# Writing out the order of an FFN's last sums and the next mixer's first tiles, moving one score span to other PSUM banks, and reordering a mixer's end

## The chip, the cores and the metric

The kernel runs on one core of one Trainium2 chip. The metric is the device time in microseconds of one execution. Before the change the median of three runs is 1155.68 us (1155.24 to 1155.77).

A core has five engines that run at the same time, each in the order of its own queue: TensorE (PE in the profile, its weight loads PEld), VectorE (DVE), ScalarE (ACT), GpSimd (POOL) and SyncE (SP), which here only sends DMAs. They wait for one another through semaphores. TensorE writes its sums to PSUM, which has eight banks of 128 partitions by 512 float32.

## The reference: what is computed

The reference is a decoder trunk of two layers on 512 tokens of width 1024. Each layer is a mixer (attention) and a gated convolutional FFN, both inside a residual with a norm ahead of it and a norm behind it:

```
h = rms_norm(x, pre_g);      x = x + rms_norm(mixer(h), post_g)
h = rms_norm(x, ffn_pre_g);  x = x + rms_norm(conv_ffn(h), ffn_post_g)
conv_ffn: u = dwconv(h @ w_up);  (silu(gate) * up) @ w_down
```

Layer 0 mixes with latent and differential attention. Layer 1 mixes with dilated attention in three head groups and with stick-breaking attention, whose scores are z = q k^T and whose weights are exp(log_sigmoid(z) + a reversed cumulative sum of log_sigmoid(-z)) below the diagonal.

## The kernel before: how the work is laid out

The 512 tokens are four rows of 128 tokens each, X[0] to X[3], held with tokens on the partitions. ORDER = (3, 2, 1, 0) is the order in which rows are finished and taken up. A normed row has to be turned (transposed by TensorE, eight 128x128 blocks in two groups of four) before it can be multiplied, since a product contracts over partitions.

Products that need precision are done in three parts. A value is split into a high part (a cast by ScalarE) and a low part (a subtraction by VectorE), and `mm3` (L259 to L263) adds high x high, high x low and low x high into one PSUM bank: three matmuls of 128x512.

**Weights.** The class `Weights` (L39) keeps a list of all weights in the order of use. `load` sends a DMA of 512 KB into one of three raw buffers, `_emit` splits it (ScalarE L73, VectorE L74) into one of five pairs wh, wl, and `next` hands out a pair after making sure that `depth` units from the present one are made.

**The planner.** Instructions are laid out on each engine by a planner with its own estimate of times, which may put a later instruction ahead of an earlier one that is not ready. Inside `tc.manual_schedule(engines={...})` the instructions that the program traces on the named engines keep the order in which they are written. SyncE is not among the named ones; and instructions that are written outside may still be put between.

**The first FFN's end** (in `ffn`, L555 to L568). The down projection is a product of 2x2 block matrices done with seven products in place of eight. Six banks are left at the end, a, b and c for two halves s = 0 and 1 of the tokens, and each takes its last TAIL = 4 units (12 matmuls). Out of a and of uu - b comes row 3 (s = 0) or row 1 (s = 1); out of uu - c and an earlier sum comes row 2 or row 0. `close` does for each row:

1. `residual` (L241): per half a square with a sum on ScalarE (L228), a product with the gain on VectorE (L223), for some halves a subtraction ahead (L220); `rstd` (L172) makes the factor on GpSimd with three operations on one column (L176, L178, L179); then the row's update on VectorE (L250).
2. `normalise` (L193): a square of the new row on ScalarE (L186), `rstd` with two operations, and two halves of the normed row on VectorE (L199).
3. `turned` (L203): per half four transposes (L209), a cast (ScalarE, L169) and a subtraction (VectorE, L170) into xh and xl.

In the kernel before this stretch is not written out: the planner lays it out.

**The second mixer** (`odd`, L1210). It starts with the value tiles of the two dilated groups (L1269 to L1283): for each row in ORDER eight `mm3` over the turned rows and four weights, a copy by ScalarE out of the bank, and four DMAs into `cv12`, sent from ScalarE's queue. The two turns that the FFN left over are popped in the middle of these tiles. Then come the stick-breaking projections (`proj_T`, L1237, and `proj_V`, L1252), whose sums go to the three banks with tag a.

`sb_scores` (L1295) makes the scores of two heads in three spans of columns. Each span has one bank per head, by tag "ss", "nt", "ss", as "s" has two banks and "n" and "t" one each; VectorE adds the mask while it empties them (L1307). `sb_softplus` and `sb_weights` follow, the last with products with a triangle (L1334), each after a few projections that fill the time.

**The mixer's end** (L1534 to L1564), in a manual order on four engines: per row two half sums of the output projection, `part_of` for each half, the row's factor and update; the square of the row before it, its normed row (L1530), and its turn come between them, one or two rows later. The FFN that follows takes rows 3 and 2 first and pops the last two turns in its first products.

The lines that the steps of the prediction touch are L73, L74 (split of a weight), L169, L170 (split of a turned half), L176 to L179 (factor), L186, L228 (squares), L199, L1530 (normed), L209 (turn), L220, L223, L250 (half row and update), L261 to L263 (`mm3`), L1283 (stores of the value tiles), L1303, L1307 (scores and mask) and L1334 (triangle).

Of the kernel before, what the change touches and what calls it, by code (L numbers as in the profile page):

```python
# [17 lines left out]
P = 128  # L18
# [20 lines left out]
class Weights:  # L39
# [35 lines left out]

    def ahead(self, n):
        while len(self.made) < min(len(self.units), n):
            self._emit()
# [9 lines left out]
def trunk(tc, A, out):  # L88
# [3 lines left out]
    with ExitStack() as top:  # L92
# [5 lines left out]
        GAP = 24  # L98
# [83 lines left out]
        def mean_square(src, eps=epst):  # L182
            w = src.shape[1]
            junk = chp.tile([P, D], BF16, tag="junk", name="junk", bufs=1)
            ms = chp.tile([P, 1], F32, tag="ms", name="ms", bufs=4)
            ACT.activation(junk[:, :w], src, AF.Square, scale=w ** -0.5, accum_out=ms[:])  # L186
            return rstd(ms[:], None, eps)
# [50 lines left out]
        def begin_sum():  # L238
            return chp.tile([P, 2], F32, tag="ms", name="ms2", bufs=4)
# [104 lines left out]
        def ffn(layer, xnT, pending, final):  # L344
            with ExitStack() as es:
# [209 lines left out]
                def close(i, cs, at=None):  # L555
                    turns.append(normalise(i, g_next, nx, "tn", residual(i, cs, g_post, None, at)))

                for s in range(2):
                    for m in "abc":
                        for n in range(TAIL):  # L560
                            later_product(m, s, HF - TAIL + n, ws[n])
                        if m == "b":
                            close(3 - 2 * s, (bk["a", s], (uu[:, s], bk["b", s])))
                        if m == "c":
                            close(2 - 2 * s, ((uu[:, s], bk["c", s]), None), early_q[s])
                        if len(turns) > 1 and s == 1 and m != "c":
                            turns.pop(0)()
                return nx, turns  # L568
# [641 lines left out]
        def odd(xnT, pending):  # L1210
            xh, xl = xnT
            with ExitStack() as es:
# [6 lines left out]
                nc.scalar.dma_start(tab12[:], A["dil_tab12"])  # L1219
# [3 lines left out]
                ob = ap.tile([P, 4, 4, 66], F32, tag="ob", name="ob")  # L1223
                on = ap.tile([P, NT, 4, 66], F32, tag="on", name="on")
# [44 lines left out]

                ws = [W.next() for _ in range(4)]  # L1270
                for i in ORDER:
                    t = slice(i * P, (i + 1) * P)
                    a = bank("a", "av12")
                    for k in range(KD):
                        if k == KD // 2 and pending:
                            pending.pop(0)()
# [3 lines left out]
                    st = sb.tile([P, 512], F32, tag="sp", name="vst", bufs=2)  # L1280
                    ACT.copy(st[:], a[:])
                    for r in range(4):
                        nc.scalar.dma_start(cv12[32 * i:32 * i + 32, r], st[r::4, :])  # L1283
# [250 lines left out]
                norms, turns = [], []  # L1534
                with tc.manual_schedule(engines={PE.engine, DVE.engine, ACT.engine, POOL.engine}):
                    for n, i in enumerate(ORDER):
# [19 lines left out]
                        turns.append(turned(i, nx, "na", t))  # L1556

                    r = mean_square(X[i][:])

                def turn_next():  # L1560
                    turns[0]()
                    normed(i, r, t)
# [106 lines left out]
```

## Time and profile before

| | |
|---|---|
| median of 3 runs | 1155.68 us |
| the profiled execution's own time | 1155.71 us |
| its span, first to last instruction | 1153.9 us |
| mean granted TensorE clock | 0.998 |
| DVE, ACT, POOL busy | 71%, 48%, 6% of the span |

How to read it: a row of the timeline has the start in us from the span's start, the length in us, the engine, the line, the operation, out<-in by the program's names, the shapes and how many instructions were merged; in brackets stands how long the engine was idle ahead of it and what ended that. A row of groups has busy time, mean ns of one, and the idle time ahead with its releasers. A row of the table of stretches has the stretch, its length, the busy time and number of instructions of PE, PEld, DVE, ACT and POOL, the granted clock, the DMA engines' busy share and GB/s. Matmuls are pipelined, so the length of one (0.39 us for 128x512) is more than the distance to the next one's start; the ends are modelled. A tile is listed under the name it was made with, digits at its end dropped: `cv12` is cv, `zp` stays zp.

### The profile page before, as it was taken

To read this page: it belongs to the slowest core of one execution; us is meant where nothing else is said; L and a number is where in the kernel's file an instruction comes from. 1 tells how busy PE (TensorE), PEld (TensorE's weight loads), DVE (VectorE), ACT (ScalarE), POOL (GpSimd) and SP (SyncE) were. 2 spreads that over 40 slices of the span, in tenths; PEclk is the share of its full clock that TensorE was granted. 3 is DMA by queue.
4 is the path that set the end of the run, shared out by engine and by line. 5 is a ranking of instruction groups with operands and counts; after the bars stand their busy time and mean duration, and the time that the engine had idled before them with its cause. 6 is when DMAs were issued, how large, how long until landed. Compare 5 with 4: busy or idle time off the path is not lost.

```text
span 1153.9 us, 15139 instructions
## 1 busy us (share of the span) xinstructions
PE 1136.1 (98%) x5632; PEld 932.3 (81%) x5632; DVE 813.9 (71%) x1435; ACT 552.2 (48%) x935; POOL 71.1 (6%) x148
## 2 busy tenths in 40 slices
PE   9999999999999999999999999999999999999997
PEld 8766677898888888888778877888988888888886
DVE  5687686568667668889863564576676666679896
ACT  5555454444434444556543554454533433445562
POOL 3200123100000000000120000002000000000002
PEclk9999999999999999999999999999999999999999
DMA  8520132153333332455635223323233333324461
GB/s 309 170 67 19 50 92 89 64 168 110 92 92 106 94 91 76 129 153 180 203 122 163 63 69 92 92 57 110 77 110 107 95 91 98 103 82 139 143 210 73
DMA packets 40921, 128.38 MB, mean 111 GB/s; under 512 B 5008, under 2 KB 7696, under 8 KB 40848
## 3 DMA queue, kind: packets, MB, share of 16 engines
q1 hardware_dynamic: 37920, 123.08, 34.2%
q10 hardware_dynamic: 2928, 4.35, 1.2%
q8 instruction: 44, 0.72, 0.3%
q14 instruction: 29, 0.24, 0.1%
HBM read 119.53 MB, written 6.29 MB: 109 GB/s over the span
## 4 chain that ended last, share of the span: by engine, by line
PE 45%; issue 2%; DVE 1%; POOL 1%; ACT 1%; POOLq 0%; DVEq 0%; ACTq 0%
PE u L262 7%; PE u L263 7%; PE u L261 7%; PE acc L261 3%; PE acc L263 3%; PE acc L262 3%; PE apt L261 3%; PE apt L262 3%; PE apt L263 3%; PE cp L1334 1%; PE apv L261 1%; PE apv L263 1%; PE apv L262 1%; PE o L1418 1%; PE o L1495 1%
## 5 line engine op out<-in xcount | busy, mean ns | idle before, releaser
L74 DVE TENSOR_TENSOR wl<-wraw,wh 128x1024 fp32r<-128x1024 f32 x176 | 213.9, 1223 | 179.3 <-ACT wh L73 174.8
L73 ACT CAST wh<-wraw 128x1024 fp32r<-128x1024 f32 x176 | 182.8, 1048 | 264.6 <-PE u L262 179.3
L262 PE MATMUL u<-xl,wh 128*128 128x512 f32 (+1 forms) x768 | 285.7, 372 | 0.1
L263 PE MATMUL u<-xh,wl 128*128 128x512 f32 (+1 forms) x768 | 285.6, 372 | 0.0
L261 PE MATMUL u<-xh,wh 128*128 128x512 f32 (+1 forms) x768 | 285.3, 372 | 0.1
L261 PEld LDWEIGHTS u<-xh,wh 128*128 128x128 f32 x768 | 144.5, 188 | 25.5 <-ACT xh L169 0.6
L262 PEld LDWEIGHTS u<-xl,wh 128*128 128x128 f32 x768 | 144.7, 188 | 25.1 <-DVE xl L170 0.3
L263 PEld LDWEIGHTS u<-xh,wl 128*128 128x128 f32 x768 | 144.7, 188 | 24.9
L262 PE MATMUL acc<-wl,gh 128*128 128x512 f32 (+1 forms) x250 | 97.0, 388 | 0.0
L263 PE MATMUL acc<-wh,gl 128*128 128x512 f32 (+1 forms) x250 | 97.0, 388 | 0.0
L261 PE MATMUL acc<-wh,gh 128*128 128x512 f32 (+1 forms) x250 | 96.9, 389 | 0.0
L415 ACT ACTIVATE y<-y 128x512 f32<-128x512 f32 x44 | 27.7, 632 | 85.3 <-DVE y L413 85.3
L410 ACT ACTIVATE y<-u,cw 128x512 f32<-128x512 f32 x88 | 67.5, 774 | 1.7 <-PE u L263 1.7
L413 DVE SCALAR_TENSOR_TENSOR y<-u,cw,y 128x510 f32<-128x510 f32 x88 | 65.6, 747 | 2.5
L411 DVE SCALAR_TENSOR_TENSOR y<-u,cw,y 128x511 f32<-128x511 f32 x88 | 65.2, 744 | 0.9 <-ACT y L410 0.9
L176 POOL TENSOR_TENSOR rv<-ms,epst 128x1 f32<-128x1 f32 x27 | 7.6, 284 | 895.9 <-ACT junk L228 843.6
L591 ACT ACTIVATE s<-s,st 128x128 f32<-128x128 f32 (+3 forms) x64 | 35.8, 559 | 45.5 <-DVE st L589 28.2
L261 PEld LDWEIGHTS acc<-wh,gh 128*128 128x128 f32 x250 | 47.0, 188 | 10.1 <-issue 0.6
L262 PEld LDWEIGHTS acc<-wl,gh 128*128 128x128 f32 x250 | 47.0, 188 | 9.6
L263 PEld LDWEIGHTS acc<-wh,gl 128*128 128x128 f32 x250 | 47.0, 188 | 9.6
L261 PE MATMUL apt<-xh,wh 128*128 128x512 f32 x128 | 50.7, 396 | 0.0
L262 PE MATMUL apt<-xl,wh 128*128 128x512 f32 x128 | 50.1, 391 | 0.0
(328 smaller groups left out, 1985.8 us busy)
## 6 DMA issues: line engine op xcount, KB each, us to landing
wraw<-in_ffn_w_up SPq DMA_DIRECT2D x88, 512.0 KB, 3.6
wraw<-in_ffn_w_down SPq DMA_DIRECT2D x44, 512.0 KB, 3.7
wraw<-in_od_w_dqk SPq DMA_DIRECT2D x12, 512.0 KB, 3.6
wraw<-in_ffn_w_down SPq DMA_DIRECT2D x22, 256.0 KB, 2.7
wraw<-in_ev_w_dqk SPq DMA_DIRECT2D x8, 512.0 KB, 3.6
wraw<-in_ev_w_out SPq DMA_DIRECT2D x8, 512.0 KB, 3.6
spill<-X SPq DMA_DIRECT2D x8, 512.0 KB, 2.8
X<-spill SPq DMA_DIRECT2D x8, 512.0 KB, 6.3
```

The costliest lines, as they stand in the source:

```text
L73: self.nc.scalar.copy(h[:, :w], raw[:, :w])
L74: self.nc.vector.tensor_tensor(l[:, :w], raw[:, :w], h[:, :w].bitcast(F32), ALU.subtract)
L261: PE.matmul(o, lh, rh, start=first, stop=False, skip_group_check=more)
L262: PE.matmul(o, lh, rl, start=False, stop=False, skip_group_check=more)
L263: PE.matmul(o, ll, rh, start=False, stop=last, skip_group_check=more)
L410: ACT.activation(y[:, z], u, AF.Identity, bias=c[:, 3:4], scale=c[:, 2:3])
L411: DVE.scalar_tensor_tensor(y[:, z, 1:], u[:, :S - 1], c[:, 1:2], y[:, z, 1:], ALU.mult, ALU.add)
L413: DVE.scalar_tensor_tensor(y[:, z, 2:], u[:, :S - 2], c[:, 0:1], y[:, z, 2:], ALU.mult, ALU.add)
L415: ACT.activation(y[:, 0], y[:, 0], AF.Silu)
L591: ACT.activation(s[:, :n], s[:, :n], AF.Exp, bias=st[:, 0:1], scale=-1.0, accum_out=st[:, 1:2])
L1334: PE.matmul(zp[:, c + (j2 - j) * P:c + n], tri[:, 0 if j2 == j else 1], part[:, off[j2]:off[j2 + 1]], start=(j2 == j and part is sh), stop ...
L1418: PE.matmul(o12[hp][:, y, r], pt[:, y, rr, g], cv12[:, r, c:c + 64], start=(g == 0), stop=(g == 1))
```

## The change

1. **One written list.** The end of the first FFN (not of the second, which has its own) becomes a list of single steps in a manual order on PE, DVE, ACT and POOL. The order stays open (an ExitStack) past the end of `ffn`, until the value tiles of the second mixer are done. The turn of row 3 stands behind the fifth of the six banks; the turns of rows 2, 1 and 0 are in the functions that `odd` pops at unit 2, 3 and 3 of its first three value tiles.
2. **Weights around it.** The depth is 4 in the tail (it was 5) and 1 in the value tiles; the fourth value weight is split by `begin` and `rest` inside the list, and each value tile but the first is followed by one weight of the coming projections. Behind the list the depth is 5 again.
3. **Buffers and DMAs.** The value tiles are copied into the tiles ob and on and stored from SyncE's queue; they were in a tile with tag sp and stored from ScalarE's. The loads of the mask, the triangle and tab12 come behind the list. Tag ms has 6 buffers for 4, and the spacer 8 columns for 24.
4. **Banks of the scores.** The third span has tag "aa" for "ss".
5. **The mixer's end.** The square of a row is written right behind its update, and the normed row ahead of the next row's second half.

```diff
+    def begin(self):
+        if len(self.raws) == len(self.made):
+            self.load()
+        h, l = self.pair()
+        self.nc.scalar.copy(h[:], self.raws[len(self.made)][:])
+        return h, l
+
+    def rest(self, begun):
+        n = len(self.made)
+        raw, self.raws[n] = self.raws[n], None
+        self.nc.vector.tensor_tensor(begun[1][:], raw[:], begun[0][:].bitcast(F32), ALU.subtract)
+        self.made.append(begun)
...
-        GAP = 24
+        GAP = 8
...
-            ms = chp.tile([P, 1], F32, tag="ms", name="ms", bufs=4)
+            ms = chp.tile([P, 1], F32, tag="ms", name="ms", bufs=6)
...
+                W.depth = 5 if final else 4
                 ws = [[W.next(), W.next()] for _ in range(TAIL)]
+                W.depth = 5
...
-                def close(i, cs, at=None):
-                    turns.append(normalise(i, g_next, nx, "tn", residual(i, cs, g_post, None, at)))
-
-                for s in range(2):
-                    for m in "abc":
-                        for n in range(TAIL):
-                            later_product(m, s, HF - TAIL + n, ws[n])
-                        if m == "b":
-                            close(3 - 2 * s, (bk["a", s], (uu[:, s], bk["b", s])))
-                        if m == "c":
-                            close(2 - 2 * s, ((uu[:, s], bk["c", s]), None), early_q[s])
-                        if len(turns) > 1 and s == 1 and m != "c":
-                            turns.pop(0)()
-                return nx, turns
...
+                order = ExitStack()
+                order.enter_context(tc.manual_schedule(engines={PE.engine, DVE.engine, ACT.engine, POOL.engine}))
+                tiles[3] = begin()
+                bank_done("a", 0)
+                times(3, lo, bk["a", 0])
+                square(3, lo, bk["a", 0])
+                bank_done("b", 0)
+                minus(3, hi, "b")
+                square(3, hi)
+                times(3, hi)
+                scale(3)
+                update(3)
+                bank_done("c", 0)
+                minus(2, lo, "c")
+                square_row(3)
+                square(2, lo)
+                normed(3)
+                times(2, lo)
+                scale(2)
+                update(2)
+                tiles[1] = begin()
+                bank_done("a", 1)
+                square(1, lo, bk["a", 1])
+                bank_done("b", 1)
+                turn(3)
+                times(1, lo, bk["a", 1])
+                square_row(2)
+                minus(1, hi, "b")
+                bank_done("c", 1)
+                square(1, hi)
+                normed(2)
+                times(1, hi)
+                scale(1)
+                update(1)
+                begun = W.begin()
+                W.rest(begun)
+                minus(0, lo, "c")
+
+                def first():
+                    turn(2)
+                    square_row(1)
+                    square(0, lo)
+                    times(0, lo)
+                    scale(0)
+                    normed(1)
+                    update(0)
+                    square_row(0)
+
+                def second():
+                    turn(1)
+                    normed(0)
+
+                return nx, [order, first, second, lambda: turn(0)]
...
-                nc.scalar.dma_start(tab12[:], A["dil_tab12"])
...
-                nc.scalar.dma_start(smask[:], A["sb_mask"])
-                nc.scalar.dma_start(trif[:], A["sb_tri"])
-                DVE.tensor_copy(tri[:], trif[:])
...
+                W.depth = 1
                 ws = [W.next() for _ in range(4)]
-                for i in ORDER:
+                made = len(W.made)
+                order = pending.pop(0)
+                for n, i in enumerate(ORDER):
                     t = slice(i * P, (i + 1) * P)
                     a = bank("a", "av12")
                     for k in range(KD):
-                        if k == KD // 2 and pending:
+                        if k == (2, 3, 3, 0)[n] and pending:
                             pending.pop(0)()
...
-                    st = sb.tile([P, 512], F32, tag="sp", name="vst", bufs=2)
-                    ACT.copy(st[:], a[:])
+                    st = o_tile(n % 2)[:].rearrange("p a b c -> p (a b c)")[:, :S]
+                    ACT.copy(st, a[:])
                     for r in range(4):
-                        nc.scalar.dma_start(cv12[32 * i:32 * i + 32, r], st[r::4, :])
+                        nc.sync.dma_start(cv12[32 * i:32 * i + 32, r], st[r::4, :])
+                    W.ahead(made + n)
+                order.close()
+                nc.scalar.dma_start(smask[:], A["sb_mask"])
+                nc.scalar.dma_start(trif[:], A["sb_tri"])
+                nc.scalar.dma_start(tab12[:], A["dil_tab12"])
+                DVE.tensor_copy(tri[:], trif[:])
+                ob, on = o_tile(0), o_tile(1)
+                W.depth = 5
...
-                        zp = [bank(t, "zp") for t in ("ss", "nt", "ss")[n]]
+                        zp = [bank(t, "zp") for t in ("ss", "nt", "aa")[n]]
...
                         part_of(t, ms, 0, acc[0], g_post, dve_first=True)
                         if n > 1:
                             turns.pop(0)()
+                        row_product(acc, terms, True, True, (1,))
                         if n:
-                            j, tj = norms.pop()
-                            rj = mean_square(X[j][:])
-                        row_product(acc, terms, True, True, (1,))
+                            normed(*last)
                         part_of(t, ms, 1, acc[1], g_post)
                         r = rstd(ms[:, 0:1], ms[:, 1:2])
-                        if n:
-                            normed(j, rj, tj)
                         DVE.scalar_tensor_tensor(X[i][:], t[:], r[:, 0:1], X[i][:], ALU.mult, ALU.add)
-                        norms.append((i, t))
+                        last = i, mean_square(X[i][:]), t
                         turns.append(turned(i, nx, "na", t))
-
-                    r = mean_square(X[i][:])
```

In the list `bank_done(m, s)` adds a bank's last four units; `minus`, `times` and `update` are the VectorE steps of L220, L223 and L250, `square` and `square_row` the ScalarE steps of L228 and L186, `scale` the three GpSimd steps of a row's factor (`square_row` has two more), `normed` the two halves of L199, and `turn` the eight transposes with their casts and subtractions.

More of the change, by code (lines that the diff above doesn't have):

```diff
@@ L238, in begin_sum @@
         def begin_sum():
[L239 removed]
+            return chp.tile([P, 2], F32, tag="ms", name="ms2", bufs=6)
         def residual(i, parts, g, dst=None, at=None):
@@ L568, in ffn, with bank_done, minus, square @@
-                return nx, turns
+                tiles, rows, scales = {2 * n: early_q[1 - n] for n in range(2)}, {}, {}
+                lo, hi = slice(0, S), slice(S, D)
+                def bank_done(m, s):
+                    for n in range(TAIL):
+                        later_product(m, s, HF - TAIL + n, ws[n])
+                def minus(i, c, m):
+                    DVE.tensor_tensor(tiles[i][0][:, c], uu[:, (3 - i) // 2], bk[m, (3 - i) // 2], ALU.subtract)
+                def square(i, c, src=None):
+                    junk = chp.tile([P, D], BF16, tag="junk", name="junk", bufs=1)
+                    n = c.start // S
+                    ACT.activation(junk[:, :S], tiles[i][0][:, c] if src is None else src, AF.Square,
+                                   scale=D ** -0.5, accum_out=tiles[i][1][:, n:n + 1])
@@ L1530, in normed @@
                         DVE.scalar_tensor_tensor(t[:, c], X[i][:, c], r[:, 0:1], g_next[:, c], ALU.mult, ALU.mult)
-                norms, turns = [], []
+                turns, last = [], None
                 with tc.manual_schedule(engines={PE.engine, DVE.engine, ACT.engine, POOL.engine}):
```

24 lines of the change are left out of this document (21 added, 3 removed).

## The prediction

> **What bounds the kernel now.** First the page's head and its busy line, then the view of waits for TensorE alone, then the table of stretches.
>
> ```profile
> span 1153.9 us, 15139 instructions
> PE 1136.1 (98%) x5632; PEld 932.3 (81%) x5632; DVE 813.9 (71%) x1435; ACT 552.2 (48%) x935; POOL 71.1 (6%) x148
> ```
> ```profile
> PE tp L209 <- DVE t L199: 2.4, 4, 1.4
> PE zp L1303 <- DVE z L1307: 1.1, 2, 0.8
> PE tp L209 <- DVE t L1530: 0.7, 1, 0.7
> ```
> ```profile
> 562.50:607.90 45.40, 42.98 (x201) 34.40 (x200) 30.76 (x41) 21.78 (x39) 10.17 (x20) 1.00 0.40 123
> 641.26:645.75 4.49, 3.54 (x18) 2.03 (x17) 4.31 (x7) 2.60 (x3) 0.00 (x0) 1.00 0.53 129
> 675.80:679.32 3.52, 3.21 (x18) 1.66 (x16) 2.79 (x6) 0.59 (x1) 0.00 (x0) 1.00 0.49 149
> ```
>
> TensorE is busy for 98% of the span at the full clock (1.00 in all three stretches), so the time is TensorE's own work plus the places where it waits. The reader should see that its three waits of interest are the places that the diff edits: the transposes (tp) of the normed rows behind the first FFN, the scores (zp) of stick-breaking, the transposes behind the second mixer. The change takes no matmul away and adds none; it can win only these waits. Busy time hides part of them, since a matmul's row is longer than the distance to the next one's start. So I go by starts.
>
> **Part 1: the written list, 562.50 to 607.90.** The stretch runs from the first of the six last banks to the first product after the value tiles.
>
> ```profile
> 562.50 0.39 PE L261 MATMUL acc<-gh 128*128 128x512 f32 x1
> ...
> 575.35 1.32 PE L209 MATMUL tp<-ident,t 128*128 128x128 f32 x8 [1.36 <-DVE t L199]
> 576.43 0.47 PE L263 MATMUL acc<-gh,gl 128*128 128x512 f32 x1
> ...
> 603.82 0.39 PE L261 MATMUL av<-wh,xh 128*128 128x512 f32 x1
> ...
> 607.90 0.39 PE L261 MATMUL apt<-xh,wh 128*128 128x512 f32 x1
> ```
>
> From 603.82 to 607.90 lie 18 undisturbed matmuls, 0.2267 us each. A bank has 4 units of 3 matmuls, 2.72 us; a value tile 8 units, 5.44 us. Eight transposes take 576.43 - 575.35 = 1.08 us, say 1.1 with the switch. Needed are 6 x 2.72 + 4 x 5.44 + 4 x 1.1 = 42.5 us; the stretch takes 45.4. **So 2.9 us are there to win.** After the change nothing in this stretch may be moved by the planner on four engines, so I walk the list with the steps that VectorE shows:
>
> ```profile
> 574.55 1.41 DVE L199 SCALAR_TENSOR_TENSOR t<-X,rr,gain 128x512 f32<-128x512 f32 x2 [1.59 <-POOL rr L179]
> 575.88 0.68 DVE L223 TENSOR_TENSOR t<-t,gain 128x512 f32<-128x512 f32 x1
> ...
> 582.58 0.68 DVE L223 TENSOR_TENSOR t<-acc,gain 128x512 f32<-128x512 f32 x1
> 583.18 0.68 DVE L223 TENSOR_TENSOR t<-t,gain 128x512 f32<-128x512 f32 x1
> ...
> 584.38 1.27 DVE L250 SCALAR_TENSOR_TENSOR X<-t,rr,X 128x1024 f32<-128x1024 f32 x1
> 585.57 0.68 DVE L170 TENSOR_TENSOR xl<-tp,xh 128x512 fp32r<-128x512 f32 x1
> ```
> ```profile
> 572.46 1.06 ACT L186 ACTIVATE junk<-X 128x1024 bf16<-128x1024 f32 x1 [2.81 <-DVE X L250]
> ```
>
> By distance of starts: a half row 0.60, an update 1.19, a normed row 1.33, a weight's low part about 1.2.
>
> - Row 3's chain up to normed keeps its order, so it ends at 575.88. TensorE's place for turn(3), now behind five banks, is 562.50 + 5 x 2.72 = 576.1: the wait of 1.36 goes.
> - turn(2), behind the sixth bank and two units: 576.1 + 1.1 + 2.72 + 1.36 = 581.3. VectorE: half row 0.60, update(2) 1.19, turn(3)'s low parts 1.20, two half rows 1.20, normed(2) 1.33 from 575.88 gives 581.4; the second four transposes need it at 581.75. Late next by 0.3 us of slack: this row.
> - The fourth value weight, now split by hand: half row, update(1), 1.2 from 581.4 gives 584.4. Its first product is at 581.3 + 1.1 + 4 x 0.68 = 585.1.
> - turn(1): 588.5 on TensorE; VectorE has normed(1) at 588.1 (a half row, turn(2)'s low parts, a half row, normed).
> - turn(0): 595.0 on TensorE. VectorE: update(0) at 589.3; turn(1)'s casts stand on ScalarE behind the square of row 0 (1.06) and a value tile's copy, which puts the low parts near 592.9, and normed(0) at 594.3.
>
> Every place is met by 0.3 to 0.7 us. The other three value weights are split ahead of the list as before, and one of the next projections' weights behind each later value tile, where nothing waits for it. I take 2.7 of the 2.9; bounds 0 and 2.9, with a loss priced as rival 4.
>
> The 16 stores of the value tiles move from ScalarE's queue to SyncE's:
>
> ```profile
> 597.34 2.61 ACTq L1283 DMA_DIRECT2D cv<-vst  x4
> ```
> ```profile
> 555.96 6.25 SPq L51 DMA_DIRECT2D wraw<-in_od_w_v  x4
> ```
> ```profile
> wraw<-in_od_w_v SPq DMA_DIRECT2D x8, 512.0 KB, 4.2
> ```
>
> Four issues held ScalarE's queue for 2.61 us. In the list ScalarE has casts of turns just behind, so the move keeps 2.61 us out of each row's chain there; it is no gain of its own. On SyncE weight loads queue behind stores; as loads run some units ahead (555.96, long before the value tiles), I cost it at nothing. The cover is gone if a load is sent only when the list reaches it (rival 1). The two more ms buffers and the spacer's 24 to 8 add no instruction; the mask and tables, loaded later now, are wanted from the first scores (641.26) on.
>
> **The rule that speaks against the list** is about GpSimd, which makes each row's factor.
>
> ```profile
> 579.26 0.19 POOL L176 TENSOR_TENSOR rv<-ms,epst 128x1 f32<-128x1 f32 x1 [3.55 <-ACT junk L186]
> 579.53 0.55 POOL L179 TENSOR_TENSOR rr<-rv,mhalf 128x1 f32<-128x1 f32 x1
> 580.78 1.27 POOL L176 TENSOR_TENSOR rv<-ms,epst 128x1 f32<-128x1 f32 x1 [0.70 <-ACT junk L228]
> ```
> ```profile
> 580.78 1.22 DVE L74 TENSOR_TENSOR wl<-wraw,wh 128x1024 fp32r<-128x1024 f32 x1
> ```
> ```profile
> L179 POOL TENSOR_TENSOR rr<-rv,mhalf 128x1 f32<-128x1 f32 x51 | 33.8, 662 | 3.8
> L176 POOL TENSOR_TENSOR rv<-ms,epst 128x1 f32<-128x1 f32 x27 | 7.6, 284 | 895.9 <-ACT junk L228 843.6 <-ACT junk L186 52.4
> L178 POOL TENSOR_TENSOR rv<-rv,ms 128x1 f32<-128x1 f32 x15 | 6.3, 417 | 16.5 <-ACT junk L228 16.2
> ```
>
> An addition of one column takes 0.19 us by itself and 1.27 beside a weight's subtraction on VectorE that starts with it and takes 1.22. A row has five such operations: three for its scale, two for its norm. On the means their excess is 2 x (0.284 - 0.19) + (0.417 - 0.19) + 2 x (0.662 - 0.55) = 0.64 us a row, part of which the chain of before had already; at 1.08 each (1.27 - 0.19) it would be 5.4. On the means a row may slip past its slack by 0.1 or so; the 0.2 that I left out of 2.9 stands for that, and the loss at 1.08 is rival 4.
>
> The Trainium skill, in SBUF — State Buffer, section "Who interferes with whom", says that a VectorE instruction with two SBUF inputs contends with a GpSimd instruction that reads SBUF, and that the one that starts first blocks the other for its whole length. The rows of 1.27 and 1.22 agree. By that rule alone, with all five behind long instructions, the list would lose.
>
> **Part 2: the third score span in other banks.**
>
> ```profile
> 644.90 0.92 PE L1303 MATMUL zp<-sq,sk 64*128 64x256 f32 x4 [0.82 <-DVE z L1307]
> ...
> 662.20 0.39 PE L1334 MATMUL cp<-sh,tri 128*128 128x512 f32 x1
> 675.80 1.77 PE L1303 MATMUL zp<-sq,sk 64*128 64x512 f32 x8
> ```
> ```profile
> 643.03 1.22 DVE L74 TENSOR_TENSOR wl<-wraw,wh 128x1024 fp32r<-128x1024 f32 x1
> ...
> 659.09 1.48 DVE L170 TENSOR_TENSOR sl<-sp,sh 128x1280 fp32r<-128x1280 f32 x1
> ```
>
> The third span waits for the banks of the first, which VectorE empties; in the first unit a weight's subtraction (643.03) stands between. The two units take 4.49 and 3.52 us. Spans one and two take about 1.65 (x8 in 1.77, its end overlapping). The third is 645.75 - 644.90 = 0.85 for one head: 0.85 if the heads run side by side, as they do in the first spans, 1.7 if not. So a unit costs 2.5 to 3.35, and the two give back 8.01 - 6.7 = 1.3 to 8.01 - 5.0 = 3.0. Behind the first unit a wait can come back: the products with the triangle (662.20) stand 1.6 us behind the end of sl (660.57), less than the 2.0 that the unit could win, so up to 0.4 returns. VectorE's mask work is unchanged. I take 2.2, the middle, since the first spans' row shows pairing and the third's a lone head; bounds 1.3 and 3.0.
>
> **Part 3: the mixer's end.** A row's square now comes right behind its update, and normed ahead of the next row's second half.
>
> ```profile
> 794.61 1.23 PE L209 MATMUL tp<-ident,t 128*128 128x128 f32 x8 [0.69 <-DVE t L1530]
> ...
> 798.20 0.39 PE L263 MATMUL ao<-wo,og 128*128 128x512 f32 x1
> 798.73 0.74 PE L261 MATMUL u<-xh,wh 128*128 128x256 f32 x4
> 799.53 0.39 PE L262 MATMUL u<-xl,wh 128*128 128x256 f32 x1
> ```
> ```profile
> 796.57 1.05 ACT L73 CAST wh<-wraw 128x1024 fp32r<-128x1024 f32 x1 [3.49 <-PE ao L263]
> ```
>
> The transposes of row 2 wait 0.7 us; moving normed ahead of one half row and the square ahead of a half's square brings them 1 us forward, so this wait goes. At the second FFN's start 0.53 - 0.23 and 0.80 - 0.48 are lost, 0.6 in all, because row 2's casts stand behind a weight's cast (796.57) on ScalarE. What is late next is that same queue: the square of row 1 (1 us) now stands ahead of those casts. So 0.1 to 0.7 + 0.6 = 1.3 us; I take 0.8. The planner lays out all that follows anew; TensorE's waits show no other line from there on, so I cost that at nothing.
>
> **Sum.** 2.7 + 2.2 + 0.8 = 5.7 us. The profiled execution's own time is 1155.71 us (span 1153.9 and 1.8 around it), 0.03 over the median of 1155.68, so the forecast is **1150.0 us**; the bounds give 1155.7 - 7.2 = 1148.5 to 1155.7 - 1.4 = 1154.3. I go 0.3 further down, for rounding in the 42.5.
>
> **Rivals.**
>
> 1. *The fourth value weight comes late.* Sent only when ScalarE gets to its place, near 581.7, it lands 4.2 later and its two halves take 1.05 and 1.2: 588.2 against 585.1, so 3.1 us lost, 1153.1. Against it: before, four such loads went out from 555.96 on.
> 2. *The banks do nothing,* as the three a banks are still held by projections: 2.2 less, 1152.2. Against it: a projection takes 5.4 us, time enough to empty one.
> 3. *The list gives nothing* (each row slips as much as the planner's order did) and the wait at the FFN's start stays: 1155.7 - 2.2 = 1153.5. For it: slacks of only 0.3 to 0.7 us.
> 4. *Slower: GpSimd behind VectorE.* If its five operations per row lose 0.64 us each, a chain is 3.2 longer, less 0.4 of slack 2.8, over three rows 8.4: 1158.4. It decides from 0.61 us each (8.0 us in all); the mean now is 0.13, which speaks against it, and the 1.08 of one row for it. Its mechanism is the rule of the Trainium skill, SBUF — State Buffer, quoted in part 1.
>
> **How the numbers follow.** Forecast 0.58 (1148.2 to 1152), rivals 0.11, 0.08, 0.11 and 0.12. A measurement tells about 0.2% from no change, 2.3 us: faster is below 1153.4, slower above 1158.0. Faster: 0.58 + 0.11 + 0.08 = 0.77; within: 0.11; slower: 0.12. The range 1148.2 to 1154.5 holds the forecast's case, rivals 1 to 3, and leaves rival 4 out.
>
> **What would show it.** Right: the stretch from the last banks to the first projection takes 42.5 to 43 us, no tp waits over 0.3 for its normed row; zp has no wait on z; the two score units take under 3.4 us each. Wrong in rival 1: a wait of av on wl's line; rival 4: additions of 128x1 over 0.8 us in the list, and tp waiting behind them. Wrong in part 3: the casts of xh before the second FFN still end after TensorE gets there.

## The result, and the profile after

The changed kernel takes 1149.0 us (median, 1148.66 to 1150.64) where the kernel before takes 1155.72 in the same measurement: a ratio of 0.9941, 95% interval 0.9924 to 0.9959. The forecast was 1150.0. Behind the edits lines have moved by 13 and more: `mm3` is L274 to L276, the turn L222, its split L182 and L183, the factor L189 to L192, the list's normed row L604 and update L596, the stores L1376, the scores L1404, the triangle L1435, the normed row of the mixer's end L1631 and its update L1652. New in the list are L583 (square), L588 (half row) and L86 (the fourth weight's low part).

The page's head and busy line of the kernel after:

```profile
span 1146.9 us, 15133 instructions
PE 1132.5 (99%) x5632; PEld 931.9 (81%) x5632; DVE 813.5 (71%) x1435; ACT 551.8 (48%) x935; POOL 70.8 (6%) x148
```

The span is 7.0 us shorter. Four stretches show where. First the table of stretches of the kernel after (the list, the two score units, the mixer's end from its first output product to the 96th matmul behind the second FFN's first), then the one row of before that the prediction did not show, the mixer's end:

```profile
562.59:605.00 42.41, 42.34 (x202) 34.66 (x200) 29.37 (x39) 19.76 (x37) 9.07 (x20) 1.00 0.43 137
638.36:640.72 2.36, 2.36 (x18) 1.47 (x17) 2.18 (x3) 2.23 (x3) 0.00 (x0) 1.00 0.10 33
670.77:673.12 2.35, 2.35 (x18) 1.46 (x16) 1.62 (x3) 0.59 (x1) 0.00 (x0) 1.00 0.59 146
762.95:805.54 42.59, 41.59 (x262) 36.63 (x262) 28.84 (x55) 18.45 (x45) 8.30 (x21) 1.00 0.27 94
```
```profile
769.09:812.55 43.46, 42.56 (x263) 36.46 (x262) 28.87 (x55) 18.45 (x45) 7.57 (x21) 1.00 0.27 93
```

Compare the length in each row (the number behind the stretch) with before: the list 45.40 to 42.41 (3.0 less), the units 4.49 to 2.36 and 3.52 to 2.35 (3.3 less together), the mixer's end 43.46 to 42.59 (0.9 less). Together that is 7.2 where the span is 7.0 shorter; 0.1 was lost again ahead of the list, which starts at 562.59 where it started at 562.50. In the first three stretches TensorE's busy time now fills the stretch to 0.1, in the fourth 1.0 is left open.

**The list.** TensorE's turns and the fourth value weight, from the timelines of TensorE and VectorE after:

```profile
576.19 1.03 PE L222 MATMUL tp<-ident,t 128*128 128x128 f32 x8
576.98 0.48 PE L274 MATMUL acc<-gh 128*128 128x512 f32 x1
...
581.22 1.29 PE L222 MATMUL tp<-ident,t 128*128 128x128 f32 x8
...
585.10 0.39 PE L274 MATMUL av<-wh,xh 128*128 128x512 f32 x1
585.53 0.50 PE L275 MATMUL av<-wl,xh 128*128 128x512 f32 x1
...
588.84 1.13 PE L222 MATMUL tp<-ident,t 128*128 128x128 f32 x8
...
595.27 1.03 PE L222 MATMUL tp<-ident,t 128*128 128x128 f32 x8
```
```profile
574.62 1.42 DVE L604 SCALAR_TENSOR_TENSOR t<-X,rr,gain 128x512 f32<-128x512 f32 x2 [1.57 <-POOL rr L192]
...
580.33 1.41 DVE L604 SCALAR_TENSOR_TENSOR t<-X,rr,gain 128x512 f32<-128x512 f32 x2
...
583.05 1.28 DVE L596 SCALAR_TENSOR_TENSOR X<-t,rr,X 128x1024 f32<-128x1024 f32 x1 [0.71 <-POOL rr L192]
584.26 1.22 DVE L86 TENSOR_TENSOR wl<-wraw,wh 128x1024 fp32r<-128x1024 f32 x1
```

The view of waits lists no turn of the list behind its normed row. But at two places the margin is gone: row 2's second half is ready at 581.74, in the middle of its turn, which takes 1.29 where the free ones take 1.03; and the fourth weight's low part ends at 585.48, 0.05 ahead of the product that reads it and 0.2 behind the 585.33 at which that product would have followed.

**The scores.** The first unit of after, and what stands behind it:

```profile
638.36 2.43 PE L1404 MATMUL zp<-sq,sk 64*128 64x512 f32 x16
```
```profile
654.59 1.48 DVE L183 TENSOR_TENSOR sl<-sp,sh 128x1280 fp32r<-128x1280 f32 x1
```
```profile
657.19 0.39 PE L1435 MATMUL cp<-sh,tri 128*128 128x512 f32 x1
```

The 16 products of two heads and three spans run in one row, with no wait on z. The triangle's products came 5.0 us earlier (662.20 before) and sl ends 4.5 us earlier (660.57 before, 656.07 now), still 1.1 us ahead of them: nothing is given back there.

**The mixer's end.** All engines' timeline where the second FFN starts, kernel after:

```profile
787.18 1.03 PE L222 MATMUL tp<-ident,t 128*128 128x128 f32 x8
...
788.69 1.06 ACT L199 ACTIVATE junk<-X 128x1024 bf16<-128x1024 f32 x1 [3.28 <-DVE X L1652]
...
789.74 1.03 ACT L73 CAST wh<-wraw 128x1024 fp32r<-128x1024 f32 x1
...
790.57 0.39 PE L276 MATMUL ao<-wo,og 128*128 128x512 f32 x1
790.68 0.58 ACT L241 ACTIVATE junk<-ao 128x512 bf16<-128x512 f32 x1
...
791.26 1.06 ACT L182 CAST xh<-tp 128x512 fp32r<-128x512 f32 x2
...
791.88 0.74 PE L274 MATMUL u<-xh,wh 128*128 128x256 f32 x4 [0.93 <-ACT xh L182]
```

Row 2's turn is done at 788.2, but its casts stand on ScalarE behind the square of row 1, a weight's cast and half a square. TensorE's last output product starts at 790.57, the next matmul 1.31 later where 0.23 would do. In TensorE's waits of after this is the one new row of the stages that the change touches; the rows of before on z and on the normed rows of the list and of the mixer's end are gone:

```profile
PE tpp L1168 <- DVE odl L183: 1.4, 1, 1.4
...
PE u L274 <- ACT xh L182: 0.9, 1, 0.9
```

### The profile page after: what moved, and what is told of

Same layout as the page of the kernel before. It is cut to its first block, busy times and chain, and to the rows that moved or that the text cites. A ratio compares the mean times of both kernels' runs of the same rounds, so it can differ in the third digit from the quotient of the medians.

```text
span 1146.9 us, 15133 instructions
## 1 busy us (share of the span) xinstructions
PE 1132.5 (99%) x5632; PEld 931.9 (81%) x5632; DVE 813.5 (71%) x1435; ACT 551.8 (48%) x935; POOL 70.8 (6%) x148
## 5 line engine op out<-in xcount | busy, mean ns | idle before, releaser
L274 PE MATMUL u<-xh,wh 128*128 128x512 f32 (+1 forms) x768 | 285.0, 372 | 0.9 <-ACT xh L182 0.9
L276 PE MATMUL u<-xh,wl 128*128 128x512 f32 (+1 forms) x768 | 285.1, 371 | 0.0
L274 PEld LDWEIGHTS u<-xh,wh 128*128 128x128 f32 x768 | 144.5, 188 | 26.1 <-ACT xh L182 1.4
L276 PEld LDWEIGHTS u<-xh,wl 128*128 128x128 f32 x768 | 144.7, 188 | 25.1
L276 PE MATMUL acc<-wh,gl 128*128 128x512 f32 (+1 forms) x250 | 96.8, 387 | 0.0
L274 PE MATMUL acc<-wh,gh 128*128 128x512 f32 (+1 forms) x250 | 96.8, 388 | 0.0
L189 POOL TENSOR_TENSOR rv<-ms,epst 128x1 f32<-128x1 f32 x27 | 5.7, 212 | 885.7 <-ACT junk L241 512.2
L274 PEld LDWEIGHTS acc<-wh,gh 128*128 128x128 f32 x250 | 47.0, 188 | 10.0 <-issue 0.6
L276 PEld LDWEIGHTS acc<-wh,gl 128*128 128x128 f32 x250 | 46.9, 188 | 9.7
L274 PE MATMUL apt<-xh,wh 128*128 128x512 f32 x128 | 50.6, 396 | 0.0
```

The source lines that it names most:

```text
L189: POOL.tensor_tensor(v[:, :n], ms, eps[:, :n], ALU.add)
L274: PE.matmul(o, lh, rh, start=first, stop=False, skip_group_check=more)
L276: PE.matmul(o, ll, rh, start=False, stop=last, skip_group_check=more)
```

## The experiments

My theory: three separate gains, each in its own stretch and each as large as TensorE's idle time there; the list's comes from the order, which meets TensorE's pace with a few tenths of slack a row, and the new end's is held down by ScalarE's queue. Rivals: the gains depend on one another; the list's gain comes from the stores; GpSimd or VectorE has become the bound of the list; edits that add no instruction count after all. Spans are compared by stretches, since each kernel's upstream part differs by up to 1 us from chip to chip.

**list_only, banks_only, end_only: one part at a time.** list_only undoes two edits of the change; banks_only and end_only are the kernel before with one edit each.

The edit of list_only against the change (it also has the mixer's end in the order of before), that of banks_only against the kernel before, and that of end_only against the kernel before:

```diff
-                        zp = [bank(t, "zp") for t in ("ss", "nt", "aa")[n]]
+                        zp = [bank(t, "zp") for t in ("ss", "nt", "ss")[n]]
```
```diff
-                        zp = [bank(t, "zp") for t in ("ss", "nt", "ss")[n]]
+                        zp = [bank(t, "zp") for t in ("ss", "nt", "aa")[n]]
```
```diff
-                        if n:
-                            j, tj = norms.pop()
-                            rj = mean_square(X[j][:])
                         row_product(acc, terms, True, True, (1,))
+                        if n:
+                            normed(*last)
                         part_of(t, ms, 1, acc[1], g_post)
...
-                            normed(j, rj, tj)
...
-                        norms.append((i, t))
+                        last = i, mean_square(X[i][:]), t
```

> The change without its banks and without its new mixer's end: the written list with its weights, buffers and DMAs alone. My theory, that the three parts act on three separate waits of TensorE, expects the stretch from the first of the six last banks to the first projection at 42.4 us, as in the changed kernel (45.4 before), the two score units at 4.5 and 3.5 as before, and a time 2.9 to 3.0 us below before, about 1152.8. The rival, that the gain of one part depends on the planner's new layout behind another, expects less than 2 or more than 4 us.

> The kernel before with the third score span in the a banks, nothing else. Separate parts expect the two score units at 2.36 us each (4.49 and 3.52 before), so 3.3 us less, about 1152.4, and no wait of the triangle products. My forecast's own value was 2.2 us with heads half paired and up to 0.4 given back at the triangle: 1153.5. The rival, banks still held by projections, expects nothing: 1155.7.

> The kernel before with the new order of the mixer's end, nothing else. Separate parts expect 0.7 to 0.9 us less, about 1154.9: the wait of the transposes on the normed row (0.69) gone, and in its place a wait of about 0.9 us of the second FFN's first products on ScalarE's casts. The rival, that this wait is the planner's layout in the changed kernel alone, expects 1.3 to 1.6 us less.

Measured on one chip: 1153.81 us, ratio 0.997 (0.9959 to 0.9981); 1153.35, ratio 0.9966 (0.9954 to 0.9978); 1156.86, ratio 0.9996 (0.9988 to 1.0005), which can't be told from no change. The stretches of list_only (list), of banks_only (two units) and of end_only (mixer's end):

```profile
562.54:604.74 42.20, 42.17 (x202) 34.66 (x200) 29.22 (x39) 19.92 (x37) 8.82 (x20) 1.00 0.43 139
```
```profile
642.98:645.34 2.36, 2.36 (x18) 1.47 (x17) 2.18 (x3) 2.23 (x3) 0.00 (x0) 1.00 0.26 26
675.40:677.76 2.36, 2.36 (x18) 1.47 (x17) 1.62 (x3) 0.59 (x1) 0.00 (x0) 1.00 0.63 153
```
```profile
770.19:813.08 42.89, 41.63 (x262) 36.65 (x262) 28.85 (x55) 18.46 (x45) 8.85 (x21) 1.00 0.27 95
```

Alone the list gives 3.2, the banks 2.13 and 1.16, the end 0.57, short of the 0.7 to 0.9 that was expected of it. So the list and the banks are separate gains, and the score units are the same to 0.01 with and without the list. The end gives 0.3 less alone than in the change, and list_only takes 0.3 off the same stretch (43.15). The sizes add up, the places do not: end_only lacks its 0.3 at the second FFN's start (1.59 from the last output product to the next matmul, 1.31 in the change), while list_only has won its 0.3 before the turn of row 2 (25.22 into the stretch, 25.52 before). Why the end gives more together with the list stays open.

**turn_first: the ScalarE queue at the second FFN's start.** In the last row's part of the mixer's end, row 2's turn is written first and the square of row 1 behind it:

```diff
+                        if n == 3:
+                            turns.pop(0)()
+                            last = last[0], mean_square(X[last[0]][:]), last[2]
                         part_of(t, ms, 0, acc[0], g_post, dve_first=True)
-                        if n > 1:
+                        if n == 2:
                             turns.pop(0)()
...
-                        last = i, mean_square(X[i][:]), t
+                        last = i, None if n == 2 else mean_square(X[i][:]), t
```

> The changed kernel, and for the last row of the mixer's end the turn of row 2 is written ahead of the half row and of row 1's square, which comes behind that turn. My theory is that the second FFN's first products now wait 0.93 us because row 2's casts stand on ScalarE behind row 1's square, which itself waits for row 1's update: it expects this wait to go and the time to fall by 0.9 to 1.2 us against the changed kernel, to about 1147.9. The rival, that the next wait (low parts on VectorE, or the turn of row 1 in the FFN) takes its place, expects 1149.

It took 1147.32 us, ratio 0.9918 (0.9906 to 0.993). Both it and the change ran again on one chip:

> The changed kernel once more, to stand on the same chip beside the next two: a ratio of 0.994 to before, as in its first runs, and a stretch of the list of 42.4 us.

> The changed kernel with row 2's turn written ahead in the mixer's end, once more, beside the changed kernel on the same chip. My theory (ScalarE's casts behind row 1's square hold up the second FFN) expects 1.0 to 1.4 us less than the changed kernel, and no wait of the FFN's first products on ScalarE. The rival, that its lead in the first runs was the chip's, expects no difference.

They took 1149.18 (0.9934; 0.992 to 0.9947) and 1148.23 (0.9924; 0.991 to 0.9937). The stretch of the mixer's end in turn_first, in change_again and in turn_first_again:

```profile
763.15:804.20 41.05, 41.05 (x262) 36.67 (x262) 28.93 (x55) 18.47 (x45) 9.57 (x21) 1.00 0.29 99
```
```profile
763.47:806.07 42.60, 41.60 (x263) 36.65 (x262) 28.83 (x55) 18.44 (x45) 8.30 (x21) 1.00 0.27 96
```
```profile
764.18:805.25 41.07, 41.07 (x262) 36.66 (x262) 28.93 (x55) 18.45 (x45) 9.51 (x21) 1.00 0.28 98
```

With the turn ahead of the square the wait is gone and TensorE is busy through the whole stretch, 1.5 us shorter in both pairs. So ScalarE's queue was the cause, and the stretch had 43.46 - 41.05 = 2.4 us to win, of which the change took 0.9. By the medians turn_first is 1.0 us under the change on that chip; the intervals of the two ratios overlap, but every run of it (1147.33 to 1148.70) is below every run of the change (1148.79 to 1149.85), and the trace shows where the time went.

The list is the same in all of these kernels. Its stretch took 42.41 in the change's first profile, 42.20 in change_again and 42.19 in turn_first_again, where the 42.4 was expected, and 42.74 in turn_first: there a weight's subtraction stood on VectorE ahead of row 3's first half row, and the turn of row 2 waited 0.3 for its normed row. A few tenths therefore differ from run to run.

**stores_act: the value tiles' stores back on ScalarE's queue.**

```diff
-                        nc.sync.dma_start(cv12[32 * i:32 * i + 32, r], st[r::4, :])
+                        nc.scalar.dma_start(cv12[32 * i:32 * i + 32, r], st[r::4, :])
```

> The changed kernel with the sixteen stores of the value tiles back on ScalarE's queue. In the changed kernel ScalarE copies the first value tile at 591.5 and casts the turn of row 1 at 592.0 to 593.1, just when TensorE wants it (592.8). My theory, that four issues hold ScalarE's queue for about 2.5 us, puts those casts 2.5 us later, so that the tile of row 1 waits 2 to 2.5 us: the stretch of the list takes 44.4 to 45 us in place of 42.4, and the time is about 1151.2. The rival, that the issues run beside ScalarE's work or that later slack takes them up, expects 42.4 to 43 and 1149.

1152.12 us, ratio 0.9949 (0.9935 to 0.9963). Its list stretch, ScalarE's timeline and the wait:

```profile
562.53:607.19 44.66, 42.74 (x202) 34.49 (x200) 28.27 (x39) 19.78 (x37) 8.82 (x20) 1.00 0.40 129
```
```profile
591.82 2.48 ACTq L1376 DMA_DIRECT2D cv<-ob  x4
594.34 1.07 ACT L182 CAST xh<-tp 128x512 fp32r<-128x512 f32 x2 [2.55 <-issue]
```
```profile
PE av L274 <- ACT xh L182: 1.9, 1, 1.9
```

The bracket says "issue": ScalarE stood 2.55 us without work while its queue sent four DMAs, and the casts of a turn behind them came late by 1.9. It is the only wait for a turn's casts that the view lists in the list: one turn of the four. The stretch is 2.25 longer than in the change, 2.46 longer than in change_again. So this order with the stores left on ScalarE gives 45.40 - 44.66 = 0.7; it needs the stores out of the way. The same four issues cost SyncE 2.46 in the kernel after, and no weight came late for them: TensorE's waits list none in the projections that follow.

**pow_thrice: has the list slack, or is GpSimd near?** The factor of each row's scale in the list does its power three times.

```diff
-            POOL.tensor_tensor(r[:, :n], v[:, :n], mhalf[:, :n], ALU.pow)
+            for _ in range(1 + again):
+                POOL.tensor_tensor(r[:, :n], v[:, :n], mhalf[:, :n], ALU.pow)
...
-                    scales[i] = rstd(ms[:, 1 - n:2 - n], ms[:, n:n + 1])
+                    scales[i] = rstd(ms[:, 1 - n:2 - n], ms[:, n:n + 1], again=2)
```

> The changed kernel, and GpSimd does the last operation of each row's scale in the list three times in place of once, on the same operands into the same result: about 1.04 us more in each of the four rows' chains. If the written places have the slack that I counted, 0.3 to 0.7 us a row, about 0.7 us is lost at the turn of row 3, nothing new at row 2 (its scale waits for VectorE anyway), about 1 us at row 1 and 0.3 at row 0: 2.0 to 2.5 us, about 1151.2. If the list has no slack at all, all four count in full: 4.2 us, 1153.2. If GpSimd's operations lie beside other work throughout, nothing: 1149.

1152.98 us, ratio 0.9957 (0.9945 to 0.997). GpSimd's row, the list stretch, TensorE's turns and its wait for the fourth weight, and VectorE's update of row 2:

```profile
570.58 1.80 POOL L193 TENSOR_TENSOR rr<-rv,mhalf 128x1 f32<-128x1 f32 x3
```
```profile
562.59:608.88 46.29, 43.30 (x202) 34.35 (x200) 29.38 (x39) 20.18 (x37) 13.54 (x28) 1.00 0.38 125
```
```profile
576.69 1.31 PE L223 MATMUL tp<-ident,t 128*128 128x128 f32 x8 [0.34 <-DVE t L605]
...
583.48 1.29 PE L223 MATMUL tp<-ident,t 128*128 128x128 f32 x8 [1.33 <-DVE t L605]
...
592.35 1.12 PE L223 MATMUL tp<-ident,t 128*128 128x128 f32 x8
...
599.12 1.03 PE L223 MATMUL tp<-ident,t 128*128 128x128 f32 x8
```
```profile
PE av L276 <- DVE wl L86: 1.3, 1, 1.3
```
```profile
578.99 1.29 DVE L597 SCALAR_TENSOR_TENSOR X<-t,rr,X 128x1024 f32<-128x1024 f32 x1 [1.09 <-POOL rr L193]
```

Three powers take 1.80 where one takes 0.55, 1.25 more a row. The stretch is 3.88 longer: more than the 2.0 to 2.5 expected with slack, less than four rows in full (5.0). The turns, which start 0.50, 2.26, 3.51 and 3.85 later than in the change, show which place pays:

- Row 3's normed row comes 1.26 later (575.88 for 574.62). The first product behind its turn is 0.78 late (577.76 for 576.98). About 0.5 of slack was there.
- Row 2: its update waits 1.09 for GpSimd, where it waited for nothing in the change; the expectation had "nothing new" here. Its normed row comes 2.25 later (582.58 for 580.33) and the turn 2.26, so this place has no slack, and the 0.5 won at row 3 is lost again.
- Row 1: the fourth weight's low part comes another 1.25 later and TensorE pays all of it. No slack here either.
- Row 0 adds 0.34 of its 1.25, near the 0.3 expected.

So the first row has about 0.5 of slack and the last 0.9; at row 2's turn and at the fourth weight there is none, where the prediction counted 0.3 to 0.7 everywhere. At these two places the list only just keeps up.

**spacer_24, spacer_16, before_8, near_128: the place of the tiles.** Four kernels in which no instruction differs; only where the tiles behind the spacer (in near_128, behind the tile lead ahead of it) lie: 64 and 32 bytes further than in the change, 64 nearer than in the kernel before, 128 nearer than in the change. The pools of X, xh and xl (glob) and of wh and wl (wpool) are opened ahead of the spacer's, those of the FFN's gh and gl behind it. So the first three kernels move gh and gl and leave xh, xl, wh and wl in place; near_128 moves all of them together.

Their edits in this order, the third against the kernel before and the others against the change:

```diff
-        GAP = 8
+        GAP = 24
```
```diff
-        GAP = 8
+        GAP = 16
```
```diff
-        GAP = 24
+        GAP = 8
```
```diff
-        lead = cst.tile([P, 80], F32, tag="lead", name="lead")
+        lead = cst.tile([P, 48], F32, tag="lead", name="lead")
```

> The changed kernel with the spacer at 24 columns as before, so that all that is laid out behind it in SBUF stands 64 bytes further. I cost the two more ms buffers and the spacer at nothing: it expects the changed kernel's time within 0.3 us and the same busy time of VectorE and ScalarE. The rival, that addresses matter to an engine's speed, expects longer instructions on VectorE, ScalarE or GpSimd and a time above by more than 1 us.

That missed: 1154.67 us beside 1149.18 for the change on the same chip (ratio to before 0.9979, 0.9971 to 0.9988). Hence the other three.

> The change with the spacer at 16 columns: everything behind it lies 32 bytes further than in the change (64 bytes less 32 against spacer_24). Theory, the place of TensorE's operands counts by 64 bytes or more: acc at 389 or 395 ns, one of the two, and the list's own waits unchanged. Rival, every shift of less than 128 bytes costs: acc over 391 ns and a span 2 to 6 us over the change's.

> The kernel before with the spacer at 8 columns: everything behind it lies 64 bytes nearer, no instruction differs. Theory, what spacer_24 lost is a matter of the operands' place modulo 128 bytes: 64 nearer is as bad as 64 further, acc takes 395 ns against 389 in the kernel before, and the span is 4 to 6 us longer. Rival, spacer_24 lost by something that only the six ms buffers or the list bring: no difference over 0.5 us.

> The change with a helper tile (lead) 32 columns narrower: everything behind it lies 128 bytes nearer, no instruction differs. Theory, the place of TensorE's operands counts modulo 128 bytes: acc at 389 to 390 ns, apt at 390 to 396, and a span within 0.7 us of the change's 1146.9 to 1147.4. Rival, the change's and the kernel before's very places are the good ones and every shift costs: acc over 391 ns and 3 to 8 us lost, as with 32 and 64 bytes.

They took 1154.53 (0.9974; 0.9963 to 0.9984), 1159.54 (1.0026; 1.0016 to 1.0035) and 1149.24 (0.9925; 0.9909 to 0.9942). One group of TensorE, the FFN's down products, in the change run again, in spacer_24, spacer_16 and near_128, and three groups in before_8 (in the kernel before the two of acc take 390 and apt, a projection's, 396):

```profile
L275 PE MATMUL acc<-wl,gh 128*128 128x512 f32 x246 | 95.7, 389 | 0.0
```
```profile
L275 PE MATMUL acc<-wl,gh 128*128 128x512 f32 x246 | 97.2, 395 | 0.0
```
```profile
L275 PE MATMUL acc<-wl,gh 128*128 128x512 f32 x246 | 97.4, 396 | 0.0
```
```profile
L275 PE MATMUL acc<-wl,gh 128*128 128x512 f32 x246 | 95.8, 390 | 0.0
```
```profile
L262 PE MATMUL acc<-wl,gh 128*128 128x512 f32 x246 | 96.9, 394 | 0.0
...
L263 PE MATMUL acc<-wh,gl 128*128 128x512 f32 x246 | 95.9, 390 | 0.0
L261 PE MATMUL apt<-xh,wh 128*128 128x512 f32 x128 | 51.3, 401 | 0.0
```

A shift of the tiles behind the spacer by 32 or 64 bytes makes groups of matmuls 4 to 7 ns longer; a shift by 32 costs as much as one by 64, as spacer_16's rival said. A shift of everything by 128 changes them by 1 ns at most. So the layout alone costs time, and the rival of near_128 (any other place costs) falls. By starts, spacer_24 and spacer_16 lose 5 us of span, mostly in the two FFNs' down products. before_8 loses 2.7 by the medians of one chip, less than the 4 to 6 expected, and 5.4 by the spans of two chips; 3.8 of the 5.4 lies behind the start of the first down product.

Two parts of the theory are not shown. One is that places count modulo 128 bytes: near_128 also keeps all distances between tiles, while the other three change those across the spacer, so it may be the distance that counts; a spacer 32 columns wider or narrower would tell. The other is that it is the place of TensorE's own operands: in before_8 apt got longer though xh and wh did not move, and the products of wh and gl stayed at 390 though gl moved. Which tiles it is, and what in the chip asks for it, stays open.

## Why the prediction was right

**The bound** (TensorE's waits in three places) held: the changed kernel wins them and little else.

**Part 1, the list**: forecast 2.7 of 2.9, measured 3.0, with TensorE's turns at 576.19, 581.22, 588.84 and 595.27 for 576.1, 581.3, 588.5 and 595.0 walked. The stretch came to the needed 42.5 within 0.1, in part by luck: the 1.1 for a turn was read off one whose second half waited. A free turn takes 576.98 - 576.19 = 0.79, and the step behind it 0.32 where 0.23 is the pace, so 0.88; the needed time is then about 168 x 0.2267 + 4 x 0.88 = 41.6 (an estimate from these rows), and the list still loses 0.8 us. The step "Every place is met by 0.3 to 0.7 us" was wrong at two places, row 2's turn and the fourth weight, where the traces leave no margin. Rival 1 fell: four loads went out from 556.22 on and the weight's cast at 581.13 waited for none; the 0.2 lost at this weight came from VectorE. "The move keeps 2.61 us out of each row's chain" held for one row's turn, not for each; stores_act puts 2.25 of the list's 3.0 on it.

**The cost at nothing of the ms buffers and the spacer** held, but only for the two together: two more buffers of 32 bytes push the tiles 64 bytes out and the spacer pulls them back. Without the spacer's edit (spacer_24) the change would have lost 5.5 us of its 7.8 on that chip. The prediction gave "add no instruction" as the reason, and that reason is not enough.

**GpSimd.** These rows of after stand beside the halves of normed(2), which VectorE runs from 580.33, and a half row from 581.65:

```profile
581.37 1.02 POOL L191 TENSOR_TENSOR rv<-rv,ms 128x1 f32<-128x1 f32 x1 [1.06 <-ACT junk L583]
582.47 0.55 POOL L192 TENSOR_TENSOR rr<-rv,mhalf 128x1 f32<-128x1 f32 x1
```

An operation of 0.19 took 1.02, and update(1) then waited 0.71 on VectorE (the row at 583.05 above). This is rival 4's mechanism at one place of the list. It did not decide: with the operation at 0.19 update(1) could have followed its half row at once, so VectorE lost 0.7 there, but of that only the 0.2 at the fourth weight reached TensorE. In change_again the same operation took 0.42 (the power behind it 0.88), and the list 0.2 less. The Trainium skill, in SBUF — State Buffer, section "Who interferes with whom", has a VectorE instruction with two SBUF inputs contend with a GpSimd one that reads SBUF; the row of 1.02 agrees, and not all five operations of a row were caught.

**Part 2, the scores**: forecast 2.2, the middle between 1.3 and 3.0; measured 3.3. This is the mis-sized term. "0.85 if the heads run side by side" was the right case: a unit takes 2.36, less than the 2.5 of that bound. And "up to 0.4 returns" at the triangle did not come, since VectorE's work moved up by 4.5 of TensorE's 5.0 us and the margin of 1.6 us took the rest. The first spans' row of before had shown the pairing (8 matmuls in 1.77); that the third span there had one head alone was a sign of the wait, not of the products.

**Part 3, the mixer's end**: forecast 0.8, measured 0.87. That these agree is luck: two terms were off against each other, and the new end alone gives 0.57. The wait of row 2's turn was taken as 0.7; from the first to the last output product the stretch shrank by 1.5 (29.11 to 27.62). From there to the 96th matmul of the FFN it grew by 0.6 (14.35 to 14.97). The text named the cause ("the square of row 1 now stands ahead of those casts"), and its sign of failure, casts of xh that end after TensorE gets there, is in the profile; turn_first shows that this queue is all of it.

**The sum** was 5.7 for a span 7.0 shorter; 1.1 of the difference is part 2, 0.3 part 1.

## What to carry to other kernels

Where TensorE is busy nearly all the time, take a stage's room from distances of starts against the pace of undisturbed matmuls, and check the queue that the new order fills: here ScalarE's held back 2.25 us in one place and 1.5 in another. A written order that meets every place on paper may have no slack at some: delay one step on purpose and read, place by place, which delay TensorE pays. When a tile's size or a buffer count changes, keep what lies behind it where it was, as the spacer did here, or compare TensorE's mean lengths before believing a time.

## What was not expected of the hardware

The place of tiles counts. Groups of TensorE's 128x512 matmuls got 4 to 7 ns longer (acc 389 to 390 ns against 394 to 396, apt 396 against 401) by a shift of 32 or 64 bytes of the tiles behind the spacer, with the granted clock at 0.998 to 0.999 in all of these kernels; a shift of everything by 128 bytes made no difference. The `u` products stayed at 389 to 390 throughout, but their operands xh, xl, wh and wl moved only in near_128, so they tell nothing of the shorter shifts. The Trainium skill, in SBUF — State Buffer, section "Operand start alignment", asks only for a multiple of the element's size, and says of itself that it is about legality and not speed; all these shifts keep to that, and the runs show that speed depends on the layout beyond it.
